# Gate stage: h added to e*gate by accumulating transfers, upper frames turned by VectorE, tiles finished one pair later

## The chip, the cores and the metric

The kernel runs on one core of a Trainium2 chip. The metric is device time in microseconds (us) of one execution. A core has five engines with an instruction queue each: TensorE (PE, with its weight loads shown as PEld), VectorE (DVE), ScalarE (ACT), GpSimd (POOL) and SyncE (SP). SP only issues transfers (DMAs); POOL issues transfers and computes as well. An engine works through its queue in order, so an instruction that waits also holds whatever stands behind it.

## The reference

One layer of a streaming encoder step over 2048 prompt frames and 32 sample frames of 1024 channels. The stage that is changed here is the last one, the gated embedding and the final norm:

```python
h = h + jnp.concatenate([yA, yB], axis=-1) @ w_out
gate = jax.nn.sigmoid(rmsnorm(h, g_ple) @ w_ple_gate)
h = h + (p @ w_ple) * gate
...
return rmsnorm(h, g_final), ...
```

All arithmetic is fp32.

## The kernel before

**Stages.** The input projection comes first, then the mixers and the output projection, then what is left of the embedding e = p·W_ple, and last the gate stage. The rows of h and of e go to device memory (`h_d`, `e_d`) and are read back by the gate stage.

**Products.** An fp32 product is done as three products in the format fp32r. `split` makes two parts of an operand: ACT copies it to fp32r (L81), and DVE subtracts that copy from the operand (L84). Two tiles of 128 frames form a pair, and a pair's [256 x 1024] times the weights' [1024 x 1024] is done as a 2x2 block matrix in seven block products (`seven`), each of 12 matmuls with a 512-wide result. Their operands are the blocks 11, 12 and 22 and the sums S1 to S4 on the side of the frames. PE does them in this order: 11, 12, S2, S1, S3, S4, 22. S1 adds the two blocks of the lower frames, S2 subtracts block 11 from S1, S3 is 11 minus 21, and S4 is 12 minus S2.

**The gate stage.** There are 16 tiles of prompt frames in eight pairs, i = 0, 2, ... 14, and tile 16 with the 32 sample frames, which runs after pair 4 ("short gate"). Pair 14 has a loop body of its own, `last_pair`. For each pair the stage needs:

- the frames turned, channels onto partitions (`prep_g`). The lower tile i+1 is loaded by quarters (four DMAs, L1512), so that a 32x32 block transposition of DVE (L1560) is all that is left to do. The upper tile i is loaded whole; ACT copies it into `ho` (L1552) and PE transposes it in eight matmuls into the PSUM tile `pth` (L1554). The sums and the splits follow (L1743, L84, L81).
- the results (`gate_ops`): ACT copies a result out of PSUM (L1573), DVE adds the second product to it (L1581), ACT takes the sigmoid (L1582, or L1579 straight from PSUM). Then DVE multiplies half a row block of e by the gate (L1584) and adds it to h (L1585).
- the finish (`done_g`): ACT squares h and sums it (L94), POOL makes the reciprocal root out of that (L73, L77), DVE scales h by it and by the final weights (L1592), and the tile is stored (L1593) by POOL for the tiles up to 5 and tile 16, else by SP.

**Buffers.** Two rings of four [128 x 1024] buffers serve the stage. `ya` holds e's rows and the frames that are to be turned (`hn`); `xh` holds h's rows. `ring4` takes the next buffer of a ring; a load into it waits until the buffer's last user is done, a store included.

**Order.** Between the seven products of pair i lie steps 1 to 6. Pair i+2 is prepared in them: at step 2 the lower frames are turned, at step 3 (step 4 for two of the pairs) the rest is made. Within what the buffers and the data allow, a scheduler places the instructions of each engine by its own estimate of the times; what is marked `keep_in_program_order` stays where the program has it. So the real order on an engine isn't that of the text, and it is shown below where it matters.

## Time and profile before

| | us |
|---|---|
| median of three runs | 911.79 (911.69 to 913.55) |
| profiled execution, its own time | 909.97 |
| its span | 908.2 |
| input projection, mixers | 0 to about 535 |
| output projection | about 535 to 705 |
| rest of the embedding | 705 to 729.5 |
| gate stage on PE | 729.5 to 900.5 |
| work after PE's last matmul | 900.5 to 908.2 |

The clock granted to PE is 0.998 of full speed in the mean. "T6" below stands for the time at which PE starts pair 6, and so on for the other pairs; in the execution before, T6 is 797.90. "T6+16.3" is 16.3 us after it.

In a row of a timeline the columns are the start, the length, the engine, the line of the kernel, the operation, result and operands, shapes and the number of instructions in the row; brackets at its end show the idle time before it and what ended that. The lengths of neighbouring instructions overlap a little, since an engine starts one while the last is draining; what one costs the engine is the distance from start to start. In a row of a group, the number of instructions stands behind the x, then the busy time and the mean in ns.

### The profile page before, as it was taken

What the parts mean: (1) busy time and instruction counts of PE and PEld (TensorE: products, weight loads), DVE (VectorE), ACT (ScalarE), POOL (GpSimd) and SP (SyncE); (2) the same over time, 40 slices, a digit from 0 to 9 for tenths busy, and PEclk for the clock granted to TensorE, in tenths of its full rate; (3) what the DMA queues carried; (4) which work ended last, traced back from release to release, by engine and by line L of the source; (5) the groups of instructions that cost most, each with busy time, mean ns of one, the idle gap of its engine ahead of it and who ended that gap; (6) DMA issues with size and microseconds to landing.
All of it is one profiled execution on the core that took longest, in us unless ns stands there. A gap on an engine that the chain in (4) does not pass through costs nothing.

```text
span 908.2 us, 12176 instructions
## 1 busy us (share of the span) xinstructions
PE 893.2 (98%) x4174; PEld 722.8 (80%) x4174; DVE 702.4 (77%) x1158; ACT 460.1 (51%) x834; POOL 152.0 (17%) x290
## 2 busy tenths in 40 slices
PE   8999999999999999999999999999999999999996
PEld 6788888888888887877778886888887888778885
DVE  6899799897993688846667579965565988897885
ACT  7744554554453345533444376544434865565554
POOL 2210122222121123100000020221111211120012
PEclk9999999999999999999999999999999999999999
DMA  8255286857699666667745496787677965565554
GB/s 268 63 188 172 84 262 204 246 157 226 179 340 424 176 222 200 215 222 225 264 136 175 163 331 198 255 259 250 199 274 254 342 244 176 184 228 196 185 193 168
DMA packets 113387, 198.52 MB, mean 219 GB/s; under 512 B 13174, under 2 KB 70062, under 8 KB 112429
## 3 DMA queue, kind: packets, MB, share of 16 engines
q1 hardware_dynamic: 91309, 124.72, 42.5%
q0 software_dynamic: 19568, 68.62, 22.2%
q10 hardware_dynamic: 2448, 4.39, 1.3%
q8 instruction: 33, 0.54, 0.3%
q14 instruction: 29, 0.24, 0.1%
HBM read 132.53 MB, written 65.15 MB: 218 GB/s over the span
## 4 chain that ended last, share of the span: by engine, by line
PE 73%; issue 11%; DMA 8%; DVE 3%; ACT 2%; POOL 2%; POOLq 0%; DVEq 0%; ACTq 0%
PE x_g L185 9%; PE x_o L185 8%; PE x_zab L646 6%; PE x_zbv L646 6%; PE x_ch L646 6%; PE z_g L185 5%; PE z_o L185 4%; DMA raw_zab_0b<-in_w_in_dram 4%; PE z_zab L646 3%; PE z_ch L646 3%; PE z_zbv L646 3%; PE e L109 2%; PE y_g L185 2%; PE y_o L185 2%; DMA B<-p_d 2%
## 5 line engine op out<-in xcount | busy, mean ns | idle before, releaser
L185 PE MATMUL z_o<-wo,y_S 128*128 128x512 f32 x192 | 47.4, 389 | 0.0
L185 PE MATMUL x_o<-wo_T,y_S 128*128 128x512 f32 x192 | 46.4, 391 | 0.6 <-DVE c_o L1319 0.6
L646 PE MATMUL x_zab<-B,w_zab_S 128*128 128x512 f32 x192 | 46.8, 392 | 0.2 <-DVE w_zab_S L84 0.2
L185 PE MATMUL z_g<-wg,g_S 128*128 128x512 f32 x192 | 46.8, 391 | 0.0
L646 PE MATMUL z_zab<-B,w_zab_S 128*128 128x512 f32 x192 | 46.8, 391 | 0.0
L185 PE MATMUL x_o<-wo,y 128*128 128x512 f32 x192 | 45.2, 390 | 0.0
L646 PEld LDWEIGHTS x_zab<-B,w_zab_S 128*128 128x128 f32 x192 | 35.8, 188 | 8.8 <-DVE w_zab_S L84 0.6
L185 PEld LDWEIGHTS x_o<-wo_T,y_S 128*128 128x128 f32 x192 | 35.9, 188 | 8.7 <-DVE c_o L1319 1.3
L185 PEld LDWEIGHTS x_o<-wo,y 128*128 128x128 f32 x192 | 36.1, 188 | 7.7
L646 PEld LDWEIGHTS z_zab<-B,w_zab_S 128*128 128x128 f32 x192 | 35.8, 188 | 7.8 <-DVE w_zab_S L84 0.3
L185 PEld LDWEIGHTS z_o<-wo,y_S 128*128 128x128 f32 x192 | 36.0, 188 | 7.5
L646 PE MATMUL x_ch<-B,w_ch_S 128*128 128x512 f32 x168 | 41.9, 393 | 0.0
L185 PEld LDWEIGHTS z_g<-wg,g_S 128*128 128x128 f32 x192 | 35.8, 188 | 7.5 <-ACT c_g L1573 0.2
L646 PE MATMUL x_zbv<-B,w_zbv_S 128*128 128x512 f32 x168 | 40.9, 393 | 0.3 <-ACT zs L986 0.3
L646 PE MATMUL z_zbv<-B,w_zbv_S 128*128 128x512 f32 x168 | 40.5, 390 | 0.0
L646 PE MATMUL z_ch<-B,w_ch_S 128*128 128x512 f32 x168 | 40.4, 390 | 0.0
L646 PEld LDWEIGHTS x_zbv<-B,w_zbv_S 128*128 128x128 f32 x168 | 31.3, 188 | 8.0 <-ACT zs L986 0.7
L646 PEld LDWEIGHTS x_ch<-B,w_ch_S 128*128 128x128 f32 x168 | 31.3, 188 | 7.3 <-ACT U L986 0.4
L646 PEld LDWEIGHTS z_ch<-B,w_ch_S 128*128 128x128 f32 x168 | 31.6, 188 | 6.6
L646 PEld LDWEIGHTS z_zbv<-B,w_zbv_S 128*128 128x128 f32 x168 | 31.5, 188 | 6.5
L81 ACT CAST y_S<-y_fS 128x512 fp32r<-128x512 f32 x28 | 17.0, 620 | 28.1 <-PE x_o L185 12.2
L1319 DVE TENSOR_TENSOR c_o<-x_o,x 128x512 f32<-128x512 f32 x14 | 9.6, 689 | 21.8 <-PE x_o L185 21.8
(552 smaller groups left out, 2288.9 us busy)
## 6 DMA issues: line engine op xcount, KB each, us to landing
wn<-in_w_in_dram SPq DMA_DIRECT2D x24, 512.0 KB, 4.8
y<-y_d SPq DMA_DIRECT2D x16, 512.0 KB, 6.8
p_dT<-T POOLq DMA_DIRECT2D x15, 512.0 KB, 5.1
e<-e_d SPq DMA_DIRECT2D x15, 512.0 KB, 4.1
x<-in_x_prompt_dram SPq DMA_DIRECT2D x14, 512.0 KB, 5.6
B<-p_d POOLq DMA_DIRECT2D x3, 2048.0 KB, 15.6
B<-p_dT POOLq DMA_DIRECT2D x3, 2048.0 KB, 21.5
h_d<-x SPq DMA_DIRECT2D x12, 512.0 KB, 7.1
```

Of the source, the lines that this page charges most:

```text
L81: ins = nc.scalar.copy(hi, src)
L109: nc.tensor.matmul(ps, pps[:, a, k], wp[k][b][:, cs], start=k + q == 0, stop=k == 1 and q == 2)
L185: nc.tensor.matmul(ps[:n], lhs[:, k, a, :n], w[b][:, k], start=start and k + q == 0, stop=k == KH - 1 and q == 2, skip_group_check=True)
L646: nc.tensor.matmul(ps, lhs[:, k, x], b[:, k, y], start=start and k + q == 0, stop=stop and k == KH - 1 and q == 2, skip_group_check=True)
L1319: add = lambda o, a, b: nc.vector.tensor_tensor(o, a, b, op=ALU.add)
```

## The change

- h's rows are not loaded any more for the pairs 0 to 12, and DVE's 28 adds (L1585 before) are gone. When both halves of a tile of e have been multiplied by the gate, POOL issues a transfer that reads the tile's 512 KB of h from `h_d` and adds them to e in place (L1590 after, `accum_op`).
- A tile is finished on e's buffer, and a pair's two tiles are finished during the next pair, at its steps 3 and 5 (in the last pair at the steps 2 and 3). `done_g`'s square and scaling are now held in program order.
- Tiles 0 to 11 and 16 are stored by POOL, tiles 12 to 15 by SP; before, SP stored the tiles from 6 on.
- e's rows of the pairs 0 to 12 move to the ring `xh`. That ring now holds a tile from the load of e to the store of the finished rows one pair later.
- The upper frames are loaded by quarters and turned by DVE as the lower ones are. ACT's copies `ho` and PE's transposes of the prompt tiles are gone. The first pair is included.
- The loads of the next pair's frames move to step 1.

```diff
-        def by_quarters(i):
+        def by_quarters(i, pool=ya):
...
-            first_h = load_rows(xh, "hn", 0, h_d)
+            first_h = by_quarters(0, xh)
...
-                ee, hh = half_of(e, at, n), half_of(h, at, n)
+                ee = half_of(e, at, n)
                 nc.vector.tensor_tensor(ee, ee, c[:n], op=ALU.mult)
-                nc.vector.tensor_tensor(hh, hh, ee, op=ALU.add)
+                if h is not None:
+                    hh = half_of(h, at, n)
+                    nc.vector.tensor_tensor(hh, hh, ee, op=ALU.add)
+                elif at[0] + at[1] == 1:
+                    r = tiles[i + at[0]][0]
+                    nc.gpsimd.dma_start(e[at[0]], h_d[r:r + P], accum_op=ALU.add)
...
-            nc.vector.scalar_tensor_tensor(h[:n], h[:n], rf[:n], g_bc[:n], op0=ALU.mult, op1=ALU.mult)
-            (nc.sync if 6 <= i < NT - 1 else nc.gpsimd).dma_start(rows_of(y_p, y_s, r, n), h[:n])
+            ins = nc.vector.scalar_tensor_tensor(h[:n], h[:n], rf[:n], g_bc[:n], op0=ALU.mult, op1=ALU.mult)
+            if later:
+                tc.keep_in_program_order(ins)
+            (nc.sync if NT - 5 <= i < NT - 1 else nc.gpsimd).dma_start(rows_of(y_p, y_s, r, n), h[:n])
...
-                got["upper"] = load_rows(ya, "hn", i, h_d) if i else first_h
+                got["upper"] = by_quarters(i) if i else first_h
...
+            def sooner():
                 if not ahead:
                     load()
-                lower.extend(turned_here(got["lower"], not i))
+
+            def first():
+                if not got:
+                    load()
+                lower.extend(turned_here(got["lower"], True))
...
-                a11, a12 = turned(i, got["upper"])
-                put("11", a11)
+                a11, a12 = turned_here(got["upper"], True)
+                put("11", a11, whole)
...
-            return {2: first, 4 if i in (2, 8) else 3: second}
+            return {1: sooner, 2: first, 4 if i in (2, 8) else 3: second}
...
-            h = [load_rows(xh, "h", i + b, h_d, queue=nc.gpsimd if i < 6 else nc.sync) for b in range(2)]
-            e = [load_rows(ya, "e", i + b, e_d) for b in range(2)]
-            seven(f"g{i}", A, W, *gate_ops(h, e, P, f"g{i}", i), following)
-            done_g(i, h[0])
+            e = [load_rows(xh, "e", i + b, e_d) for b in range(2)]
+            if i:
+                following = joined(following, finish)
+            seven(f"g{i}", A, W, *gate_ops(None, e, P, f"g{i}", i), following)
+            finish = {st: lambda b=b, i=i, e=e: done_g(i + b, e[b], True) for b, st in enumerate((3, 5))}
             if i in (0, 2, 4):
                 next(short_steps)
-            if i + 2 < NT - 3:
-                done_g(i + 1, h[1])
-        last_pair(NT - 3, S[NT - 3], lambda: done_g(NT - 4, h[1], True))
+        last_pair(NT - 3, S[NT - 3], finish[3], finish[5])
```

Three places show how the order moves. The first is DVE in pair 6, from the end of the short gate to the first split of pair 8. The names: `c_g6_11` is the gate of pair 6's block (1,1), `hn_9` and `hn_8` are the lower and the upper frames of pair 8, `g8_11` is its operand 11 (low part), `g8_fS1` the sum S1. A row "TENSOR_SCALAR e_3" is the finish of tile 3, and "TENSOR_TENSOR e_5<-e_5,c_g4_11" a multiplication of tile 5 by the gate. Before:

```order
L1581 TENSOR_TENSOR c_g6_00_7193<-y_g6_7179,c_g6_00_7193 128x512
L1560 STREAM_TRANSPOSE hn_9_7211<-hn_9_7211 128x1024
L1592 TENSOR_SCALAR h_16_6917<-h_16_6917,rstd_f16_7158,g_bc_89 32x1024
L1592 TENSOR_SCALAR h_5_6931<-h_5_6931,rstd_f5_7166,g_bc_89 128x1024
L1584 TENSOR_TENSOR e_6_7174<-e_6_7174,c_g6_00_7193 128x512
L1743 TENSOR_TENSOR g8_fS1_7247<-hn_9_7211 128x512
L1585 TENSOR_TENSOR h_6_7170<-h_6_7170,e_6_7174 128x512
L84 TENSOR_TENSOR g8_11_7263<-pth_8_0_7249,g8_11_7263 128x4x128
```

After, in the same stretch of DVE:

```order
L1584 TENSOR_TENSOR e_5_6873<-e_5_6873,c_g4_11_6982 128x512
L1597 TENSOR_SCALAR e_3_6682<-e_3_6682,rstd_f3_7003,g_bc_89 128x1024
L1584 TENSOR_TENSOR e_5_6873<-e_5_6873,g_g4_10_7035 128x512
L1581 TENSOR_TENSOR c_g6_11_7177<-x_g6_7100,c_g6_11_7177 128x512
L1581 TENSOR_TENSOR c_g6_01_7155<-z_g6_7102,c_g6_01_7155 128x512
L1584 TENSOR_TENSOR e_6_7096<-e_6_7096,c_g6_00_7115 128x512
L1560 STREAM_TRANSPOSE hn_9_7117<-hn_9_7117 128x1024
L1597 TENSOR_SCALAR e_4_6871<-e_4_6871,rstd_f4_7161,g_bc_89 128x1024
L1750 TENSOR_TENSOR g8_fS1_7179<-hn_9_7117 128x512
L1560 STREAM_TRANSPOSE hn_8_7122<-hn_8_7122 128x1024
L1584 TENSOR_TENSOR e_7_7098<-e_7_7098,c_g6_11_7177 128x512
L1750 TENSOR_TENSOR g8_fS2_7185<-g8_fS1_7179,hn_8_7122 128x512
```

The split of `g8_11` comes next. What was eight rows behind the first result of pair 6 now stands behind the results (1,1) and (0,1), behind the multiplications of the tiles 5, 6 and 7 and behind the finishes of the tiles 3 and 4.

The second place is POOL in the same pair. Its rows are the stores (L1600), the accumulating transfers (L1590) and the small steps of the roots (L73, L77). After:

```order
L1600 DMA out_0_dram<-e_2_6680 128x1024
L73 TENSOR_SCALAR ms_f16_7090<-ssq_f16_7088 32x1
L77 TENSOR_TENSOR rstd_f16_7092<-ms_f16_7090,nhalf_83 32x1
L1600 DMA out_1_dram<-h_16_6867 32x1024
L73 TENSOR_SCALAR ms_f4_7159<-ssq_f4_7157 128x1
L77 TENSOR_TENSOR rstd_f4_7161<-ms_f4_7159,nhalf_83 128x1
L1600 DMA out_0_dram<-e_3_6682 128x1024
L1590 DMA e_5_6873<-h_d_58 128x1024
L1600 DMA out_0_dram<-e_4_6871 128x1024
L73 TENSOR_SCALAR ms_f5_7226<-ssq_f5_7224 128x1
```

The sample rows take one place in the ring `xh`, which shifts it by one: the load of e's tile 5 follows the store of tile 2, that of tile 6 the store of tile 16, that of tile 7 the store of tile 3, and from there on the load of tile k+4 the store of tile k. All these stores are rows of POOL, and an accumulating transfer stands in one queue with them.

The third place is SP from the last preparation on. Before:

```order
L396 DMA e_14_7900<-e_d_59 128x1024
L396 DMA h_14_7902<-h_d_58 128x1024
L396 DMA h_15_7904<-h_d_58 128x1024
L129 DMA pps_l_7898<-pp_d_65 128x512
L123 DMA wl_0_0_7925<-wl_d00_61 128x1024
```

After:

```order
L396 DMA e_14_7770<-e_d_59 128x1024
L396 DMA e_10_7432<-e_d_59 128x1024
L396 DMA e_11_7434<-e_d_59 128x1024
L396 DMA e_12_7600<-e_d_59 128x1024
L396 DMA e_13_7602<-e_d_59 128x1024
L129 DMA pps_l_7768<-pp_d_65 128x512
L123 DMA wl_0_0_7795<-wl_d00_61 128x1024
L123 DMA wl_0_1_7796<-wl_d01_62 128x1024
L123 DMA wl_1_0_7799<-wl_d10_63 128x1024
L123 DMA wl_1_1_7800<-wl_d11_64 128x1024
L396 DMA h_14_7772<-h_d_58 128x1024
L396 DMA h_15_7774<-h_d_58 128x1024
```

The loads of h for the last pair move behind the loads of its other operands (`pps_l`, `wl`); their buffers are those of the tiles 10 and 11, which are stored in the last pair itself.

More of the change, by code (lines that the diff above doesn't have):

```diff
@@ L1611, in short_ops, with last_pair @@
             return carry, out
-        def last_pair(i, A, before):
+        def last_pair(i, A, sooner, before):
             pps = load_pps(ss.tile([P, 2, 2, P], F32R, tag="s", name="pps_l"), i + 1, nc.sync)
@@ L1728, in end @@
                 normed(1, root(1))
-            seven(f"g{i}", A, W, held, out, {1: chunk, 3: before, 4: rest, 5: upper_half}, first_tile=True, end=end)
+            seven(f"g{i}", A, W, held, out, {1: chunk, 2: sooner, 3: before, 4: rest, 5: upper_half}, first_tile=True, end=end)
         def prep_g(i, ahead=False):
@@ L1739, in put, with comb @@
                 split(view(A[q][:, :, 0]), view(A[q][:, :, 1]), src)
-            def comb(q, x, y, op, view=lambda t: t):
-                t = ss.tile([P, KH, P], F32, tag="s", name=f"g{i}_f{q}")
-                nc.vector.tensor_tensor(view(t), x, y, op=op)
+            def comb(q, x, y, op):
+                t = whole(ss.tile([P, KH, P], F32, tag="s", name=f"g{i}_f{q}"))
+                nc.vector.tensor_tensor(t, x, y, op=op)
                 return t
@@ L1749, in load @@
                 got["lower"] = by_quarters(i + 1) if i else first_lower
[L1750 removed]
+                got["upper"] = by_quarters(i) if i else first_h
             if ahead:
                 load()
[L1755 removed]
+            def sooner():
                 if not ahead:
                     load()
[L1758 removed]
+            def first():
+                if not got:
+                    load()
+                lower.extend(turned_here(got["lower"], True))
             def second():
                 a21, a22 = lower
[L1762 to L1764 removed]
+                s1 = comb("S1", a21, a22, ALU.add)
+                a11, a12 = turned_here(got["upper"], True)
+                put("11", a11, whole)
                 s2 = comb("S2", s1, a11, ALU.subtract)
[L1766 to L1768 removed]
+                s3 = comb("S3", a11, a21, ALU.subtract)
+                put("12", a12, whole)
+                put("S2", s2, whole)
                 s4 = comb("S4", a12, s2, ALU.subtract)
[L1770 to L1772 removed]
+                put("S1", s1, whole)
+                put("S3", s3, whole)
+                put("S4", s4, whole)
                 put("22", a22, whole)
             S[i] = A
[L1776 removed]
+            return {1: sooner, 2: first, 4 if i in (2, 8) else 3: second}
         S = {}
@@ L1806, in short_gate, with joined, both, run @@
             yield
+        def joined(a, b):
+            def both(p, q):
+                def run():
+                    p()
+                    q()
+                return run
+            return {**a, **{st: both(a[st], f) if st in a else f for st, f in b.items()}}
         short_steps = short_gate()
```

10 lines of the change are left out of this document (1 added, 9 removed).

## The prediction

> **What bounds the kernel now.** I read the page's busy shares first, then the stage's windows, PE's timeline in a pair, the groups of the gate stage, and the transfers.
>
> ```profile
> PE 893.2 (98%) x4174; PEld 722.8 (80%) x4174; DVE 702.4 (77%) x1158; ACT 460.1 (51%) x834; POOL 152.0 (17%) x290
> ```
>
> PE bounds the whole span. One row per pair of the gate stage gives length, then busy time of PE, PEld, DVE, ACT and POOL, the granted clock, the share of the DMA engines and GB/s:
>
> ```profile
> 797.90:817.80 19.90, 19.90 (x92) 16.32 (x91) 18.19 (x28) 12.66 (x22) 4.23 (x7) 1.00 0.69 231
> 817.80:837.90 20.10, 20.10 (x94) 16.71 (x94) 14.89 (x22) 9.22 (x17) 1.98 (x4) 1.00 0.59 212
> 837.90:858.00 20.10, 20.10 (x94) 16.53 (x93) 17.05 (x25) 11.70 (x21) 2.07 (x4) 1.00 0.58 210
> 858.00:878.30 20.30, 20.30 (x96) 16.78 (x94) 15.94 (x24) 10.36 (x20) 2.15 (x4) 1.00 0.50 173
> ```
>
> PE is busy through every pair at full clock, DVE for 15 to 18 of 20 us. So in this stage the time is what PE executes, plus whatever PE comes to wait for. Between pairs lies one piece of other work, the short gate:
>
> ```profile
> 790.53 1.08 PE L337 MATMUL x_gl<-wg,gl_a 128*64 128x512 f32 x4
> 797.90 2.90 PE L185 MATMUL x_g<-wg,g 128*128 128x512 f32 x12
> ...
> 803.36 2.88 PE L185 MATMUL x_g<-wq,g_S 128*128 128x512 f32 x12
> 806.08 2.88 PE L185 MATMUL z_g<-wg,g_S 128*128 128x512 f32 x12
> 808.81 1.03 PE L1554 MATMUL pth<-ident,ho 128*128 128x128 f32 x8
> 809.60 3.02 PE L185 MATMUL x_g<-wg_T,g_S 128*128 128x512 f32 x12
> ...
> 878.06 0.63 PE L185 MATMUL x_g<-wg,g 128*128 128x512 f32 x2
> ```
>
> A block product takes 2.72 us from start to start (803.36 to 806.08), seven take 19.04. From T6 = 797.90 to T14 = 878.06, four pairs take 20.04 each. The short gate covers 7.4 us ahead of T6.
>
> **The gain.** The difference, 1.00 us a pair, is PE's transposition of the upper frames (0.79 from start to start in the rows above, the rest in the products around it). The groups of the stage:
>
> ```profile
> L1554 PE MATMUL pth<-ident,ho 128*128 128x128 f32 x56 | 7.4, 274 | 0.0
> L1585 DVE TENSOR_TENSOR h<-h,e 128x512 f32<-128x512 f32 x28 | 18.8, 685 | 0.8 <-DMA h<-h_d 0.6
> L1592 DVE SCALAR_TENSOR_TENSOR h<-h,rstd_f,g_bc 128x1024 f32<-128x1024 f32 x14 | 18.0, 1283 | 9.2 <-POOL rstd_f L77 9.2
> L94 ACT ACTIVATE junk<-h 128x1024 bf16<-128x1024 f32 x14 | 14.8, 1057 | 4.3 <-DVE h L1585 2.2 <-issue 2.0
> L1560 DVE STREAM_TRANSPOSE hn<-hn 128x1024 f32<-128x1024 f32 x7 | 8.7, 1238 | 0.0
> L1552 ACT COPY ho<-hn 128x512 f32<-128x512 f32 x14 | 8.1, 619 | 3.1 <-DMA hn<-h_d 3.1
> L1573 ACT COPY c_g<-x_g 128x512 f32<-128x512 f32 x16 | 9.2, 577 | 4.7 <-PE x_g L185 4.7
> L1582 ACT ACTIVATE c_g<-c_g,rs_h 128x512 f32<-128x512 f32 x21 | 14.7, 718 | 15.2 <-DVE c_g L1581 15.2
> L81 ACT CAST g_S<-g_fS 128x512 fp32r<-128x512 f32 x30 | 17.3, 617 | 13.4 <-DVE g_fS L1743 13.4
> L77 POOL TENSOR_TENSOR rstd_f<-ms_f,nhalf 128x1 f32<-128x1 f32 x14 | 8.1, 576 | 1.1
> L73 POOL TENSOR_SCALAR ms_f<-ssq_f 128x1 f32<-128x1 f32 x14 | 6.4, 455 | 110.1 <-ACT junk L94 110.0
> ```
>
> Seven groups of eight matmuls lie in these 56, an eighth at the start of the stage; all go, so −8.0 us on PE (0.79 each would be −6.3, the lower end). On DVE a pair loses four additions and gains one transposition, on ACT it loses two copies; neither engine bounds the stage, so this brings nothing by itself. Both frames come by quarters now, so SP issues three more transfers a pair (24 with the first), and drops eight of its ten loads of h and six of its eight stores. POOL drops 6 loads of h, gains 14 accumulating transfers, and stores 13 tiles instead of 7. SP's and POOL's issuing is a cost only through what waits behind it.
>
> **The new waits.** Steps on DVE cost this from start to start:
>
> ```profile
> 824.33 1.28 DVE L1592 SCALAR_TENSOR_TENSOR h<-h,rstd_f,g_bc 128x1024 f32<-128x1024 f32 x1 [0.72 <-POOL rstd_f L77]
> 825.53 0.68 DVE L1581 TENSOR_TENSOR c_g<-y_g,c_g 128x512 f32<-128x512 f32 x1
> ...
> 827.61 1.24 DVE L1560 STREAM_TRANSPOSE hn<-hn 128x1024 f32<-128x1024 f32 x1
> 828.77 0.65 DVE L1585 TENSOR_TENSOR h<-h,e 128x512 f32<-128x512 f32 x1
> ...
> 833.34 0.68 DVE L1743 TENSOR_TENSOR g_fS<-g_fS,pth 128x512 f32<-128x512 f32 x1
> 833.94 0.68 DVE L1743 TENSOR_TENSOR g_fS<-pth,hn 128x512 f32<-128x512 f32 x1
> ```
>
> A finish costs 1.2, a transposition 1.16, any operation on half a tile 0.6. The transfers, with the KB of one and the median us from issue to landing:
>
> ```profile
> e<-e_d SPq DMA_DIRECT2D x15, 512.0 KB, 4.1
> ...
> h<-h_d POOLq DMA_DIRECT2D x6, 512.0 KB, 5.2
> out_dram<-h POOLq DMA_DIRECT2D x6, 512.0 KB, 3.6
> e_d<-eout POOLq DMA_DIRECT2D x2, 512.0 KB, 5.8
> ```
>
> A buffer of `xh` becomes free when its tile is stored, and only then is the next e loaded. One round trip r is a store of POOL, 3.6, a load, 4.1, and 0.2 of handing over: 7.9. Before, the loads ran a pair ahead; now the trip lies behind a finish that is itself made a pair later. The accumulating transfer (L) isn't in the trace. Its nearest row is POOL's plain load of the same 512 KB of h, 5.2, which I take; POOL's store, 3.6, is the low end, twice the load, 10.4, the high one, since it has to read the tile it adds to.
>
> *Pair 6 to 8.* PE ends the short gate at T6. Behind its last product ACT has a copy, a sigmoid and two casts (0.6 to 0.7 each) and the square of tile 2 (1.06). Then come POOL's root (0.46 + 0.58) and DVE's finish (1.2): T6+6. Ahead of the store POOL's queue also holds the root of tile 3. I put the store at T6+7.0. Tile 5 of e is there at 7.0+r. In the order after, DVE then has: multiply tile 5 (0.6), finish tile 3 (1.2), whose store goes out at T6+8.9+r and whose buffer tile 7 of e needs. Tile 7 lands at 8.9+2r; multiplication, S2 and the split of `g8_11` (0.6 each) make it 10.8+2r with the handover to PE. Pair 8 should start at 19.04, so PE waits 2r−8.2. There is a second path, over the multiplication of tile 5: ACT's copy of the next result uses the gate's buffer that it frees, PE's S4 product waits for that copy (8.3+r), ends 2.72 later, and 7.1 us of DVE rows follow up to the split: 18.2+r, a wait of r−0.8. At r = 7.9 the first decides: **+7.6**. Even with no transfer late, S4 ends at T6+16.3 and the same 7.1 us follow (three results and products 1.8, two transpositions 2.3, one finish 1.2, three more 1.8): a floor of +4.6. Before, `g8_11` stood ahead of these results.
>
> The pairs 0 to 4 have no predecessor in the ring or only an early one. At T4 the preparation of pair 6 ends about T4+21.2 by the same rows, and the short gate keeps PE until T4+26.4: nothing. In the pairs 8 and 10 the preparation stands ahead of the late rows: nothing.
>
> *Pair 12 to 14.* Tile 8 is finished at about T12+6.3: sigmoid, two casts with their splits, square, root, finish, 5.4 by the rows, and some handovers. Its store goes out at 6.4, tile 12 of e lands at 6.4+r; DVE then has five operations of 0.6 (three of them the last sums and the split), two transpositions and another result, 6.0 in all: 12.4+r against 19.04, so r−6.6, **+1.3**.
>
> *The last pair.* Before, its own h was loaded long ahead:
>
> ```profile
> 891.02 0.69 DVE L1634 TENSOR_TENSOR h<-h,c_g 128x512 f32<-128x512 f32 x1
> ...
> 894.99 0.69 DVE L1670 TENSOR_TENSOR c_g<-x_g,c_g 128x512 f32<-128x512 f32 x1
> ...
> 900.58 0.42 DVE L1633 TENSOR_TENSOR g_l<-e_l,g_l 128x256 f32<-128x256 f32 x1 [0.39 <-PE e_l L109]
> ```
>
> The first addition came at T14+13.0, the last result was added up by T14+17.5 (895.60), and PE's last four short products follow that. Now the rows of h wait for the store of tile 10, which is finished at about T14+8.5, so they land at 8.6+r = 16.5. There is also the square of tile 13, on ACT ahead of the copy that PE's S4 product needs. The accumulating transfer of tile 13 goes out at T14+7.1, square and copy follow it, so S4 starts at 8.9+L and its result is added at 12.3+L = 17.5. The later of the two counts. Behind it DVE has that addition, two finishes and two more operations: 4.2 to 17.5+4.2 = 21.7 instead of 17.5, **+4.2**. In general the term is max(8.6+r, 12.3+L)−13.3; that is 3.2 with r alone.
>
> **The sum:** −8.0 + 7.6 + 1.3 + 4.2 = +5.1. On the profiled execution, 909.97, that is 915.1. The median of the runs stands 1.8 above that execution, so for it I forecast 911.79 + 5.1 = **916.9**.
>
> **Rivals.** *Light transfers, no change.* The single landings in this stage spread widely:
>
> ```profile
> DMA to landing us min/median/max: 2.3/3.9/6.9
> ```
>
> If stores and accumulating transfers came near the light end, some 3.3 us each, with r = 6.7, pair 8 would wait 5.9 (second path), pair 14 0.1, the end 8.6+6.7−13.3 = 2.0 or, by L, 12.3+3.3−13.3 = 2.3: −8.0+5.9+0.1+2.3 = +0.3, or 912.1. For it: the DMA engines are busy for 0.50 to 0.69 of these pairs, and most loads of h leave SP. Against: the medians above come from the same stage at the same traffic. The Trainium skill, DMA: Bandwidth & Descriptors, section "Anatomy of one DMA — SWDGE (gpsimd) path", gives 2.0 us plus bytes over 436e3 per us for a transfer issued by GpSimd, which for 512 KB would be an estimated 3.2 us and bring the sum to about zero; the trace's medians of 3.6 to 5.8 on POOL's queue lie above it, so I keep the trace's.
>
> *Faster.* The place is POOL's stores of the tiles 2, 8 and 10. If they went out 3 us earlier than I count (the handovers and the root ahead of them are my weakest numbers), pair 8 would wait the floor, 4.6, pair 14 nothing, the end max(13.5, 14.5)−13.3 = 1.2: −8.0+4.6+1.2 = −2.2, or 909.6. From there on it is faster by more than 0.2%, which is 1.8 us and about what a measurement of this kernel can tell from no change. Against: the floor rests on the order and on PE's own times.
>
> *The accumulating transfer is slow.* At L = 10.4, the square of tile 5 on ACT, which stands ahead of the cast of `g8_11`, decides: its multiplications end at T6+9.5+r, and L, the square, cast and split (2.3) follow, so pair 8 waits r+L−7.3 = 11.0, and the end waits 9.4: −8.0+11.0+1.3+9.4 = +13.7, or 925.5. For it: it reads and writes the tile. Against: POOL's other transfers of this size land in 3.6 to 5.8. The Trainium skill, SBUF — State Buffer, section "SBUF: two separate sides", says that a VectorE operation in a two-port mode keeps GpSimd from writing the descriptors of its transfers; POOL's stores land sooner here (3.6) than the loads of SP (4.1) with DVE busy for 17 of 20 us, so the trace shows none of it.
>
> **How the numbers follow.** The forecast's own case (two to three waits of this size, 914 to 922) 0.56; light transfers 0.15; faster 0.11; slow accumulating transfer 0.12; another wait that I don't see, slower, 0.06. Faster by over 0.2%: 0.11, within 0.2% 0.15, slower 0.74. The range 910.5 to 927 leaves out most of the faster case and what lies above the slow transfer.
>
> **What would show it.** No `pth` of 128x128 in the gate stage, and pairs of 19.04 us on PE wherever nothing waits. An idle PE of 7 to 8 us ahead of pair 8, with DVE waiting for transfers of e's tiles 5 and 7; about 1 ahead of pair 14; an end of the last pair that is some 4 us longer. L is read as the time from issue to landing of the accumulating transfer. I am wrong if PE goes from pair 6 to 8 without a gap, if L is near 10 or more, or if a wait opens in the pairs 0 to 4.

## The result and the profile after

The changed kernel takes 943.53 us in the median (940.25 to 946.42), the kernel before 912.08 beside it: 1.034 times as long, 95% interval 1.0314 to 1.0366. The forecast, 916.9 with a range to 927.0, had the direction, but a sixth of the size: +5.1 us where +31 were measured. The profiled execution after is the longest of the six, 946.42 with a span of 944.6, 36.4 us above the span before.

The page's busy shares and the transfers of the gate stage, as they stand now:

```profile
PE 900.6 (95%) x4110; PEld 723.0 (77%) x4110; DVE 695.2 (74%) x1138; ACT 453.0 (48%) x818; POOL 165.3 (17%) x304
```

```profile
e<-e_d SPq DMA_DIRECT2D x15, 512.0 KB, 4.4
hn<-h_d SPq DMA_DIRECT2D x57, 128.0 KB, 5.8
e<-h_d POOLq DMA_DIRECT2D x14, 512.0 KB, 6.9
out_dram<-e POOLq DMA_DIRECT2D x12, 512.0 KB, 5.1
```

Two things are to be seen. PE has 64 matmuls fewer, 8.0 us by the prediction's count, and is busy 7.4 us longer: its other matmuls took some 15 us more in all. And it stands idle for 944.6−900.6 = 44.0 us where it was 15.0, 29 more. So 29 us of waits and 15 us of slow matmuls, less 8, make up the 36. In the median the accumulating transfers land after 6.9 us, POOL's stores after 5.1 instead of 3.6, the quarters of the frames after 5.8 instead of 2.9.

Where the time went, pair by pair. T is the start of a pair as PE would have it without waits inside its first two products (the start of its third product less 5.44 us); pair 4 includes the short gate:

| stretch | before | after | more | the prediction had |
|---|---|---|---|---|
| start to T0 | 729.5 | 736.7 | +7.2 | −1 |
| T0 to T2 | 20.0 | 19.0 | −1.0 | −1.0 |
| T2 to T4 | 21.1 | 19.9 | −1.2 | −1.0 |
| T4 to T6 | 27.4 | 32.0 | +4.6 | −1.0 |
| T6 to T8 | 20.2 | 31.1 | +10.9 | +6.6 |
| T8 to T10 | 19.9 | 19.4 | −0.5 | −1.0 |
| T10 to T12 | 20.1 | 21.1 | +1.0 | −1.0 |
| T12 to T14 | 20.0 | 24.6 | +4.6 | +0.3 |
| T14 to the end | 30.1 | 40.7 | +10.6 | +4.2 |

**Pair 6 to 8** is the place that the prediction worked out in most detail. The rows of the timeline after, of POOL, SP, DVE, ACT and PE (start, length, engine):

```profile
813.69 0.62 POOL L1600 DMA_DIRECT2D out_dram<-e  x1
816.82 0.34 SPq L396 DMA_DIRECT2D e<-e_d  x1
821.49 0.69 DVE L1584 TENSOR_TENSOR e<-e,c_g 128x512 f32<-128x512 f32 x1 [3.42 <-DMA e<-e_d]
822.27 0.59 ACT L1573 COPY c_g<-z_g 128x512 f32<-128x512 f32 x1 [4.63 <-DVE e L1584]
822.91 3.01 PE L185 MATMUL z_g<-wg,g_S 128*128 128x512 f32 x12 [1.73 <-ACT c_g L1573]
823.68 0.63 POOL L1600 DMA_DIRECT2D out_dram<-e  x1 [3.82 <-DVE e L1597]
824.31 0.91 POOL L1590 DMA_DIRECT2D e<-h_d  x1
828.82 0.34 SPq L396 DMA_DIRECT2D e<-e_d  x1
832.93 1.22 PE L185 MATMUL x_g<-wg,g 128*128 128x512 f32 x2 [4.29 <-ACT g L81]
835.13 0.69 DVE L1584 TENSOR_TENSOR e<-e,c_g 128x512 f32<-128x512 f32 x1 [3.40 <-DMA e<-e_d]
837.08 4.63 PE L185 MATMUL x_g<-wg,g 128*128 128x512 f32 x10 [2.07 <-DVE g L84]
```

The chain is the one foretold. The store of tile 2 (813.69) lets the load of e's tile 5 go (816.82), its multiplication follows at 821.49: the first round trip took 7.8 us. The store of tile 3 (823.68) lets tile 7 go at 828.82, and it is multiplied at 835.13: the second took 11.4, with an accumulating transfer issued right behind the store. Its store took 5.1 us (to 828.82) and what follows 6.3, where 3.6 and 4.1 had been taken. The two paths over S4 and over `g8_11` are both there as waits of PE: 1.73 at 822.91, and 4.29 and 2.07 for the two parts of `g8_11` at 832.93 and 837.08. The 4.29 ends with ACT's cast, which stands behind the square of tile 5, and that square waited for its accumulating transfer: the path of the rival with the slow transfer. DVE had turned the upper frames only 0.5 us before that cast, so this path added no more than that.

**Pair 4 to 6** was put down as free of waits:

```profile
780.12 1.77 POOL L1590 DMA_DIRECT2D e<-h_d  x2
781.78 0.67 POOL L1600 DMA_DIRECT2D out_dram<-e  x1
791.30 0.34 SPq L396 DMA_DIRECT2D e<-e_d  x1
795.38 0.69 DVE L1584 TENSOR_TENSOR e<-e,c_g 128x512 f32<-128x512 f32 x1 [5.21 <-DMA e<-e_d]
803.90 1.29 PE L337 MATMUL x_gl<-wg,gl_a 128*64 128x512 f32 x4 [3.56 <-DVE c_gl L1608]
```

The load of e's tile 4 needs the buffer of tile 1. That tile's store stands behind two accumulating transfers in POOL's queue and is done 9.5 us after its issue (781.78 to 791.30). The trip is 13.6 us, DVE waits for it, and the short gate, which was to cover the preparation, itself waits for a row of DVE behind it.

**Pair 12 to 14** lost 4.6 us by a trip of the same kind. POOL stores tile 8 at 885.64; tile 12, which takes its buffer, is multiplied 11.3 us later:

```profile
896.92 0.69 DVE L1584 TENSOR_TENSOR e<-e,c_g 128x512 f32<-128x512 f32 x1 [7.60 <-DMA e<-e_d]
899.40 4.62 PE L185 MATMUL x_g<-wq,g 128*128 128x512 f32 x12 [3.74 <-DVE c_g L1581]
```

PE's wait stands ahead of the last product of pair 12, which waits for a result that DVE adds behind that multiplication; the prediction had it ahead of pair 14. Pair 10, put down as free, has two smaller waits of PE around its end, 0.94 and 0.45.

**Slow matmuls.** The columns of the windows are length, busy time of PE, PEld, DVE, ACT, POOL, granted clock, DMA share, GB/s:

```profile
832.90:837.00 4.10, 2.08 (x4) 1.16 (x4) 1.87 (x4) 1.04 (x3) 0.40 (x1) 0.50 0.57 201
837.00:842.00 5.00, 4.92 (x12) 3.85 (x13) 4.84 (x8) 1.47 (x4) 0.00 (x0) 0.50 0.35 109
842.00:855.00 13.00, 13.00 (x58) 10.75 (x57) 9.63 (x14) 5.88 (x11) 2.40 (x3) 0.99 0.86 211
...
899.40:904.00 4.60, 4.60 (x13) 3.64 (x14) 4.60 (x8) 3.58 (x7) 0.00 (x0) 0.63 0.02 9
904.00:917.80 13.80, 10.90 (x49) 8.68 (x47) 9.35 (x14) 7.07 (x13) 4.77 (x9) 0.98 0.80 216
917.80:921.70 3.90, 2.08 (x4) 1.16 (x4) 0.00 (x0) 1.65 (x4) 1.35 (x4) 0.50 0.98 362
921.70:927.10 5.40, 5.35 (x13) 4.25 (x14) 0.00 (x0) 0.00 (x0) 0.45 (x1) 0.50 0.58 209
```

After such a gap PE doesn't start again at full clock: it is granted about half for some 3 to 4 us, and for 5 behind the second of two gaps (the windows from 837.0 and 921.7). The ten matmuls at 837.08 take 4.4 us from start to start; at full clock, with 2.72 for twelve, ten take 2.3. The prediction had no such term.

**The last pair.** SP, ACT and PE, in order of time:

```profile
906.35 6.18 SPq L123 DMA_DIRECT2D wl<-wl_d  x4
916.21 1.06 ACT L94 ACTIVATE junk<-e 128x1024 bf16<-128x1024 f32 x1 [4.84 <-DMA e<-h_d]
917.26 0.57 ACT L1573 COPY c_g<-x_g 128x512 f32<-128x512 f32 x1
917.88 2.08 PE L185 MATMUL x_g<-wg_T,g_S 128*128 128x512 f32 x4 [2.98 <-ACT c_g L1573]
920.07 1.06 ACT L94 ACTIVATE junk<-e 128x1024 bf16<-128x1024 f32 x1 [2.24 <-DMA e<-h_d]
921.13 0.57 ACT L1573 COPY c_g<-z_g 128x512 f32<-128x512 f32 x1
```

Both squares wait for their accumulating transfers, and the two copies behind them are those that PE's products S3 (917.88, a gap of 2.98) and S4 (921.75, 1.79) wait for. POOL issued the transfers at 907.98 and 910.54, 8.2 and 9.5 us before the squares began. They ran beside the four loads of `wl`, 512 KB each, which SP issues from 906.35 on; in the window from 917.8 the DMA engines are busy for 0.98.

### The profile page after: what moved, and what is told of

Its sections match the earlier page's. It is cut to its first block, busy times and chain, and to the rows that moved or that the text cites. A ratio compares the mean times of both kernels' runs of the same rounds, so it can differ in the third digit from the quotient of the medians.

```text
span 944.6 us, 12042 instructions
## 1 busy us (share of the span) xinstructions
PE 900.6 (95%) x4110; PEld 723.0 (77%) x4110; DVE 695.2 (74%) x1138; ACT 453.0 (48%) x818; POOL 165.3 (17%) x304
## 5 line engine op out<-in xcount | busy, mean ns | idle before, releaser
L185 PE MATMUL z_g<-wg,g_S 128*128 128x512 f32 x192 | 49.2, 406 | 3.5 <-ACT c_g L1573 3.5
L1584 DVE TENSOR_TENSOR e<-e,c_g 128x512 f32<-128x512 f32 x21 | 14.2, 685 | 31.9 <-DMA e<-e_d 28.7
L185 PE MATMUL x_g<-wg,g 128*128 128x512 f32 x96 | 27.3, 433 | 6.4 <-ACT g L81 4.3
```

Source lines behind the costliest of these rows:

```text
L185: nc.tensor.matmul(ps[:n], lhs[:, k, a, :n], w[b][:, k], start=start and k + q == 0, stop=k == KH - 1 and q == 2, skip_group_check=True)
L1584: nc.vector.tensor_tensor(ee, ee, c[:n], op=ALU.mult)
```

## The experiments

Each verdict is against the kernel before, timed on the same chip in the same stretch; its median lay between 910.6 and 912.2 us. Where no other figure is given, the number in brackets is the 95% interval of the ratio.

### Which part carries the loss

**The upper frames alone (e1).** The change's part on the upper frames is put into the kernel before:

```diff
-                got["upper"] = load_rows(ya, "hn", i, h_d) if i else first_h
+                got["upper"] = by_quarters(i) if i else first_h
...
-                a11, a12 = turned(i, got["upper"])
+                a11, a12 = turned_here(got["upper"], True)
```

> The kernel before with one part of the change alone: the upper frames are loaded by quarters and turned by VectorE, pair 0 included; h is loaded and added, and tiles are finished, as before. Theory A (the loss comes from e's buffers, which wait for stores of the next pair): the gate stage gains 1.0 us a pair, 8.0 in all, and loses about 4 ahead of pair 0, where PE waits for transfers that stand behind the quarters of the first upper tile in SP's queue: about 908. Theory B (the quarter loads crowd SP's queue and hold the stage): slower than before, 918 or more, with PE waiting in the pairs.

Measured: 937.51 us against 911.21, a ratio of 1.029 (1.0261 to 1.0313). This part, which I had booked as pure gain, loses 26 us by itself, as theory B has it. It isn't quite the part as the change has it: here the frames are loaded at step 2 as before, there at step 1.

**The same but for pair 0 (e2).**

> As the one with the upper frames alone, but pair 0's upper tile is loaded whole and turned by PE as before. If the wait ahead of pair 0 comes from the three more transfers at that place, it goes: about 905, some 3 us below the other, and PE starts pair 0 at 729.5 again. If it comes from elsewhere, the two are equal but for the 0.8 us of PE's transposition.

Measured: 931.27, 1.022 (1.0198 to 1.0234), 6 us less than e1. PE's part of the embedding, from its first product to T0, takes 23.8 us in e1 and 24.9 in e2, so the three transfers of the first tile are not where the 6 us lie: T0 differs by 1.5, and most of the rest falls on pair 2 (25.3 to 19.9 us), whose order of DVE changed too. That expectation failed.

The cause shows in e1 itself, between the pairs 8 and 10:

```profile
840.32 3.18 SPq L1512 DMA_DIRECT2D hn<-h_d  x6
854.05 1.28 DVE L1592 SCALAR_TENSOR_TENSOR h<-h,rstd_f,g_bc 128x1024 f32<-128x1024 f32 x1 [0.72 <-POOL rstd_f L77]
855.25 1.24 DVE L1560 STREAM_TRANSPOSE hn<-hn 128x1024 f32<-128x1024 f32 x1
857.19 1.22 PE L185 MATMUL x_g<-wg,g 128*128 128x512 f32 x2 [8.50 <-ACT g L81]
```

The quarters are issued by 843.5, but the planner has put the turning of the upper frames behind both finishes of pair 8. In DVE's order the split of `g10_11` stands 15 and 12 rows behind the results (1,1) and (0,1); before, it stands 8 and 9 rows ahead of them. PE waits 8.5 us for the operand.

**The quarters in ACT's queue (e5).** Against e2:

```diff
-                got["upper"] = by_quarters(i) if i else first_h
+                got["upper"] = by_quarters(i, queue=nc.scalar) if i else first_h
```

> As the kernel with the upper frames turned by VectorE but for pair 0, and the quarters of the upper tile are issued by ACT instead of SP. The arithmetic and the buffers are the same. Theory D (the transposition by VectorE cost so much because its loads stood in SP's queue, and the planner put the turning behind the pair's results): the preparation of each pair stands ahead of the result (1,1) again, PE goes from pair to pair without a gap, seven pairs gain 1.0 each: 903 to 907. Theory E (VectorE's own extra time, or the 128 KB transfers themselves, cost it): no better than before, 911 or more.

Measured: 924.61 against 912.24, 1.015 (1.0128 to 1.0168). E2's loss falls from 20 to 12 us with one word, and the order comes back: the split of `g10_11` stands ahead of both results again. So the queue was a cause, as theory D has it, but not the only one; the time lies in theory E's range. What is left are waits like this, in e5's timeline:

```profile
774.05 4.62 PE L185 MATMUL x_g<-wq,g 128*128 128x512 f32 x12 [3.11 <-DVE c_g L1581]
845.13 4.56 PE L185 MATMUL x_g<-wq,g 128*128 128x512 f32 x12 [3.12 <-DVE c_g L1581]
```

PE's product 22 waits for a result that DVE adds only behind the preparation, which is now longer (theory E's part; that this is why the result is late is argued from the order, and no run isolates it), and both times the product then runs at reduced clock.

**The rest of the change without the upper frames (e3).** The upper frames are loaded whole and turned by PE as before; the diff is that of e1 the other way round.

> The changed kernel with the upper frames loaded whole and turned by PE as before; accumulating transfers, finish in the next pair and buffers as in the change. Theory A: nearly all of the loss stays, 940 to 948, with PE's gaps around pairs 6, 8 and 14. Theory B: 915 or less.

Measured: 934.16, 1.026 (1.0236 to 1.0277), between the two theories. Each of the two halves of the change alone costs 23 to 26 us, both together 31, but not in the same pairs. T4 to T6 is 33.6 us here, T6 to T8 25.1, the end 35.5. e1 loses its time mostly in the pairs 2, 8 and 12 (25.3, 30.7 and 27.4 us) and none at the end; the changed kernel, which loads the frames a step earlier, has 19.9 and 19.4 in the pairs 2 and 8. So e1's 26 us are not what the upper frames cost in the changed kernel. That is the distance from e3 to it, 9 us instead of a gain of 8: in the profiled executions T6 to T8 is 6.0 us longer than in e3, T12 to T14 3.9, the end 5.3, while every other pair is 0.5 to 1.7 shorter.

### The accumulating transfers

**Finished in the same pair (e4).**

```diff
-            finish = {st: lambda b=b, i=i, e=e: done_g(i + b, e[b], True) for b, st in enumerate((3, 5))}
+            done_g(i, e[0])
+            if i + 2 < NT - 3:
+                done_g(i + 1, e[1])
+            finish = {3: lambda: None, 5: lambda e=e: done_g(NT - 4, e[1], True)}
```

(and `finish` is not joined to the steps of the next pair any more.)

> The changed kernel with one thing undone: a pair's tiles are finished directly behind their pair, not at the next pair's steps. The accumulating transfers and e's buffers stay as they are. Theory A (buffers held too long): the stores come some 8 us earlier, the loads of e with them, and most gaps close: 915 to 925. Theory C (the accumulating transfers and POOL's queue make the round trip long, wherever the finish stands): 935 or more.

Measured: 938.71, 1.029 (1.0261 to 1.0316). The gain against the changed kernel is 5 us, in theory C's range; theory A asked for some 20. That the finish comes a pair later is not the main cause. PE's waits are spread over all pairs but the first now, for results on DVE or ACT's copies of them.

**The transfer without the addition (e6).** It writes h over e, so the sum is left out; every engine's order is that of the changed kernel.

```diff
-                    nc.gpsimd.dma_start(e[at[0]], h_d[r:r + P], accum_op=ALU.add)
+                    nc.gpsimd.dma_start(e[at[0]], h_d[r:r + P])
```

> The changed kernel with the addition left out of the accumulating transfers: the same 14 transfers write h's rows over e, in the same queue and order, so that the output is h and not h + e*gate. Every instruction order is that of the changed kernel. Theory F (the addition makes the transfer long, 6.9 us instead of about 5, and the waits with it): 6 to 12 us less than the changed kernel, 931 to 937. Theory G (the place and the queue cost it, whatever the transfer does): within 3 of it, 941 to 946.

Measured: 934.83, 1.026 (1.0229 to 1.0296), 9 us less than the changed kernel, as theory F has it.

**Eight rows instead of 128 (e10).** Again every order is the same:

```diff
-                    nc.gpsimd.dma_start(e[at[0]], h_d[r:r + P], accum_op=ALU.add)
+                    nc.gpsimd.dma_start(e[at[0]][:8], h_d[r:r + 8], accum_op=ALU.add)
```

> The changed kernel, but each accumulating transfer moves 8 rows instead of 128 (32 KB instead of 512): the same instructions in the same order with the same waits; h is left out of the sum for all other rows. Theory J (the bytes of the transfer cost it, its length and what it takes from the stores and loads beside it): 915 to 922, near the kernel without transfers. Theory K (the dependence and the place in POOL's queue cost it): 930 or more, near the kernel with the plain transfers.

Measured: 921.58 against 911.01, 1.012 (1.0090 to 1.0140), at the upper end of theory J's range.

**No transfer (e7).** The `elif` with the transfer is taken out; the order changes a little.

> The changed kernel without its 14 accumulating transfers: h is left out of the sum for the tiles 0 to 13. What is left of the loss are the buffers held until the next pair's stores, the quarters in SP's queue and the order. Theory A (held buffers): 925 to 935, still with gaps ahead of the pairs 6 and 8. Theory F or G (the transfers carry the loss): 905 to 915.

Measured: 917.12, 1.007 (1.0043 to 1.0090), between the two ranges and nearer to that of F and G.

The transfers in the three of them, with KB and us to landing, e6 first, then e10 (e7 has none), and below it the stores of e7:

```profile
e<-h_d POOLq DMA_DIRECT2D x14, 512.0 KB, 5.3
```

```profile
e<-h_d POOLq DMA_DIRECT2D x14, 32.0 KB, 3.3
```

```profile
out_dram<-e POOLq DMA_DIRECT2D x12, 512.0 KB, 3.4
```

The steps from the changed kernel down are the clearest thing in this study, since every engine's order is the same in the first three: 943.5 with the addition (6.9 us a transfer), 934.8 without it (5.3), 921.6 with a sixteenth of the bytes (3.3), 917.1 with none. So the bytes of the transfer and its addition carry 22 of the 31 us, and the dependence and the place in the queue 4 to 5. About 5 us of the loss remain without any transfer. The profiled executions say the same of the gate stage alone: from T0 to the end of PE's last matmul they take 200.6 us in the changed kernel, 190.0 in e6, 179.9 in e10, 175.0 in e7 and 171.0 before. Pair 4 to 6 shows it best, with 32.0, 28.7, 26.8 and 26.4. Theory J holds against K for the sum, and F against G. The price that the prediction took for the transfer, POOL's plain load with 5.2 us, was right for the plain transfer (5.3) and too low for the accumulating one. The Trainium skill, DMA: Bandwidth & Descriptors, section "Anatomy of one DMA — SWDGE (gpsimd) path", would give an estimated 3.2 us for each 512 KB; the trace has 6.9, 5.3 without the addition, and 3.4 for stores where no such transfer is about.

The last pair is the exception. From T14 to the end of PE's last matmul it takes 33.5 us in the changed kernel, 31.1 in e6, 29.0 in e10, 24.4 in e7 and 22.4 before. Its two transfers land after 8.1 and 9.4 us, without the addition after 7.2 and 7.5, and with 32 KB still after 6.4 and 5.2, each time beside the loads of `wl`. So there the wait for a transfer at that place (theory K) carries more than its addition or its bytes. That the loads of `wl` make the transfers long is the likely reason, and no run has moved them.

**All stores by SP (e8).**

```diff
-            (nc.sync if NT - 5 <= i < NT - 1 else nc.gpsimd).dma_start(rows_of(y_p, y_s, r, n), h[:n])
+            (nc.sync if i < NT - 1 else nc.gpsimd).dma_start(rows_of(y_p, y_s, r, n), h[:n])
```

> The changed kernel with all stores of the prompt tiles issued by SP, so that a store doesn't stand behind an accumulating transfer in POOL's queue. Theory H (the round trip is long because stores queue behind accumulating transfers): the store's time falls from 5.1 to about 3.5 and the kernel gains 4 us or more, 940 or less. Rival: in SP's queue the stores hold the loads that stand behind them: 945 or more.

Measured: 943.40, 1.035 (1.0323 to 1.0380), no different from the changed kernel and between the two ranges. The stores did become fast (3.0 us in the median), so half of theory H is right, but the time came back at other places: T12 to T14 is 25.1 us and the end 43.4, with a single wait of 7.2 us for ACT's copy behind the squares, and the accumulating transfers took 7.9.

### What a gap costs

**Waits put in by hand (e9).** Into the kernel before:

```diff
                 s1 = comb("S1", a21, a22, ALU.add, whole)
+                for _ in range({4: 3, 8: 5, 10: 7, 12: 9}.get(i, 0)):
+                    nc.vector.tensor_tensor(s1, s1, s1, op=ALU.max)
```

> The kernel before with waits put in by hand: ahead of the sums of pairs 4, 8, 10 and 12 VectorE has 3, 5, 7 and 9 more operations of 0.6 us (each takes the maximum of S1 with itself, so that nothing is changed). Theory I (a gap of PE costs more than its length, since the granted clock falls to half after one of some 2.5 us): the products behind a short gap take 2.72 us as ever, those behind a longer gap 4.2 or more, and the kernel loses 1.5 us or more beyond its gaps. Rival: 12 matmuls take 2.72 us behind every gap, and the loss is the sum of the gaps.

Measured: 924.53 (two runs), 1.014 (1.0117 to 1.0170). PE's rows behind the largest gap, and the windows around it and around the last one:

```profile
850.96 1.22 PE L185 MATMUL x_g<-wq,g_S 128*128 128x512 f32 x2 [4.07 <-ACT g_S L81]
851.98 1.05 PE L185 MATMUL z_g<-wg,g_S 128*128 128x512 f32 x2
852.83 3.13 PE L185 MATMUL x_g<-wq,g_S 128*128 128x512 f32 x10
855.80 2.43 PE L185 MATMUL z_g<-wg,g_S 128*128 128x512 f32 x10
```

```profile
850.90:855.00 4.10, 4.04 (x11) 3.04 (x12) 4.10 (x7) 1.56 (x4) 0.00 (x0) 0.59 0.81 268
855.00:860.00 5.00, 5.00 (x28) 4.24 (x27) 4.96 (x9) 3.75 (x8) 0.00 (x0) 1.00 0.98 347
...
892.30:897.00 4.70, 4.67 (x15) 3.74 (x16) 4.17 (x7) 2.36 (x5) 0.00 (x0) 0.69 0.30 118
```

Behind the gap of 4.07 us the clock is 0.59 over the next 4.1 us, a loss of 1.7; behind three gaps of 1.28, 0.87 and 1.43 in a row it is 0.69 over 4.7 us, another 1.5. Of the 12.2 us by which the gate stage and its end grew (190.9 to 178.7), 8.3 are gaps and 3.9 aren't. Theory I holds in kind. Across all profiles of this study, 12 matmuls behind a single gap of up to 1.78 us took 3.0 to 3.3 us, but once 4.5 (behind 1.64, in e1); behind gaps of 1.81 to 3.12 mostly 4.2 to 4.6, but three times 3.0 (behind 2.61, 2.89 and 3.11); behind 3.7 and more always 4.4 or more. So the length of a gap alone doesn't decide it. Two gaps of 1.57 and 0.55 us in a row brought the clock to 0.65 over 4.5 us in e15, and 1.49 and 0.55 in e14 left it at 1.00; what else counts stays open. The Trainium skill, TensorE: Matmul & The Clock Gate, section "Part 1: The HAM clock gate (the "warmup" mystery)", has this rule: after an idle window of some 3.4 us the clock falls to half, and it takes about as long to be released. The length of the slow stretch agrees; the gaps that set it off begin lower here, at 1.6 to 1.8 us.

### Is the gain real

**Two additions by GpSimd (e11) and one (e12).** In the kernel with ACT's queue, to take off DVE what it had gained; e11 loads the frames one step earlier too:

```diff
-                nc.vector.tensor_tensor(hh, hh, ee, op=ALU.add)
+                (nc.gpsimd if n == P and at[0] == at[1] else nc.vector).tensor_tensor(hh, hh, ee, op=ALU.add)
```

> The kernel before with the upper frames of pairs 2 to 14 turned by VectorE, their quarters issued by ACT, the loads one step earlier, and two of the four additions of h a pair (blocks (0,0) and (1,1)) made by GpSimd. Theory L (what was left of the loss in the ACT-queue kernel is VectorE's time between the results and the next preparation, 1.2 us more a pair): the gaps ahead of the product 22 close, 903 to 908. Rival: GpSimd's additions, 1.3 us each, are late or slow VectorE, and it stays at 915 or more.

> As the kernel with the upper frames turned by VectorE and their quarters issued by ACT, and one addition of h a pair, that of block (0,0), made by GpSimd. Theory L: half of the gaps ahead of the product 22 go, 908 to 918. Rival: no change against that kernel, 922 or more.

Measured: e11 917.20, 1.006 (1.0046 to 1.0082); e12 927.29, 1.017 (1.0150 to 1.0192), no better than e5. Both lie in their rival's range. In e11 the pairs 8 and 10 take 19.0 and 19.1 us, the gain whole; the loss sits in the pairs 0, 4 and 6. In pair 0, ACT stands for 6.0 us behind the copy of the sample frames, whose load is late in SP's queue.

**Only some pairs on VectorE (e13, e14, e15).** Upper frames of the pairs 10 and 12, then 4 as well, then 14 as well, the additions of the pair ahead on GpSimd:

```diff
-                got["upper"] = load_rows(ya, "hn", i, h_d) if i else first_h
+                got["upper"] = (by_quarters(i, queue=nc.scalar) if i in DV else load_rows(ya, "hn", i, h_d)) if i else first_h
```

> The kernel before with the upper frames of the pairs 10 and 12 alone turned by VectorE (quarters issued by ACT), and the additions of the blocks (0,0) and (1,1) of the pairs 8 and 10 made by GpSimd. If the gain of 1.0 us a pair is real: 909 to 910, the pairs 8 and 10 take 19.04 us on PE. If VectorE's longer preparation gives it back: equal to the kernel before or slower, 911 to 914.

> The same with pair 4 as well (and GpSimd's additions in pair 2). Gain real: 908 to 909, three pairs of 19.04. Given back: 911 to 915.

> The same with the pairs 4, 10, 12 and 14. Gain real and no wait ahead of pair 14: 907 to 908. A wait ahead of pair 14 as in the kernel with all pairs on VectorE (20.9 us there): 909 to 911.

Measured: 917.06 (1.0054, 1.0036 to 1.0071), 913.89 (1.0026, 1.0013 to 1.0039), 915.65 (1.0043, 1.0027 to 1.0058). All slower, e13 and e15 by more than either of their two cases, e14 within "given back". Pair 2 gains 1.2 us in e14 (21.1 to 19.9), but pair 8 takes 23.0 instead of 19.9, with three waits:

```profile
834.66 0.73 PE L185 MATMUL x_g<-wg,g 128*128 128x512 f32 x2 [1.49 <-ACT g L81]
835.94 2.56 PE L185 MATMUL x_g<-wg,g 128*128 128x512 f32 x10 [0.55 <-DVE g L84]
839.56 3.02 PE L185 MATMUL x_g<-wq,g 128*128 128x512 f32 x12 [1.05 <-DVE c_g L1583]
```

**The same with the loads one step earlier (e16, e17).**

```diff
-            return {2: first, 4 if i in (2, 8) else 3: second}
+            return {**({1: sooner} if i in DV else {}), 2: first, 4 if i in (2, 8) else 3: second}
```

> The kernel of e14 (the upper frames of the pairs 4, 10 and 12 turned by VectorE, two additions a pair of the pairs 2, 8 and 10 on GpSimd) with the loads of these pairs' frames one step earlier. Gain real, lateness was the cause: the pairs 2, 8 and 10 take 19.0 to 19.9 us, 908 to 909, faster than the kernel before by 0.3%. If VectorE's time gives it back wherever the loads stand: 911 or more.

> The same with pair 14 as well: 907 to 909 if the wait ahead of pair 14 goes too, 909 to 911 if it stays (20.9 us in e11).

Measured: e16 910.87, a ratio of 1.0003 (0.9983 to 1.0022), no change; e17 909.03 against 910.55, 0.9976 (0.9962 to 0.9989). Pair 8 takes 19.0 us in both, so the lateness was the cause there. e17 is faster than the kernel before, by 0.24%: of four pairs at 1.0 us, 1.5 us are left. Its time lies where its two ranges meet, and the wait ahead of pair 14 stayed. PE's waits in its gate stage:

```profile
814.97 3.06 PE L185 MATMUL x_g<-wq,g 128*128 128x512 f32 x12 [0.27 <-DVE c_g L1583]
852.75 3.01 PE L185 MATMUL x_g<-wq,g 128*128 128x512 f32 x12 [0.27 <-DVE c_g L1583]
873.67 3.04 PE L185 MATMUL x_g<-wq,g 128*128 128x512 f32 x12 [1.56 <-DVE c_g L1583]
```

The last, ahead of pair 14, is the only one over 0.3 us.

## Why the prediction was wrong

The sum came out 31 us too low in the profile (36.4 measured, 5.1 forecast). By place that is 8.2 us ahead of T0, 5.6 in pair 4, 4.3 in pair 6, 2.5 in the pairs 8 and 10, 4.3 in pair 12 and 6.4 in the last pair; the pairs 0 and 2 came as foretold. The steps that failed are the prices of the transfers: r = 7.9 and L = 5.2 were taken from a trace without accumulating transfers, and with them the trips that held PE up took 11.3 to 13.6 us (one stayed at 7.8) and the transfers 5.2 to 9.4. Pair 4 and the clock behind a gap were put at nothing. One by one:

- **The gain of 8.0 us**: right in size. Where nothing waits, a pair takes 19.0 us (T0 to T2 after; the pairs 8 and 10 of e11; pair 8 of e17). The step that failed is the sentence behind it, that neither DVE nor ACT bounds the stage, "so this brings nothing by itself", and that SP's and POOL's issuing costs only "through what waits behind it". I counted the transfers and followed what waited in a few places only. Against e3 the upper frames cost the changed kernel 9 us instead of bringing 8; in the kernel before they cost 26 (e1), and 12 with their quarters in ACT's queue and pair 0 left as it was (e5). There, quarters late in the plan put the preparation behind the pair's results (e1), and with the order restored PE still waits for results that DVE adds behind the longer preparation (e5).
- **Pair 6 to 8, +7.6**: the chain held, row for row. The store of tile 2 came at T6+6.05 (7.0 foretold), the first trip took 7.8 us (7.9), the second 11.4. With these the formula gives 6.05+3.8+7.8+11.4 = 29.1 less 19.04, a wait of 10.0; that and about 2 us of reduced clock are the 12.0 us by which T6 to T8 exceeds 19.04. The failing term is r for a store with an accumulating transfer beside it.
- **"The pairs 0 to 4 have no predecessor in the ring or only an early one"**: wrong, and a wait there was one of the prediction's own signs of being wrong. Tile 4's load waited for tile 1's store, 13.6 us in all, since two accumulating transfers stood ahead of it. With 32 KB in each of these (e10) the stretch takes 26.8 us instead of 32.0.
- **Pair 12 to 14, +1.3**: the store of tile 8 came at T12+6.4 as foretold; the trip took 11.3 us instead of 7.9. The formula gives 4.7 with it, 5.6 was measured, and PE's product 22 ahead of pair 14 ran at a clock of 0.63.
- **The last pair, +4.2**: the path over the squares decided, as foretold, with L of 8.2 and 9.5 instead of 5.2. Its formula gives 8.5 with 9.5; the rest to 10.6 is again the clock (0.50 in the windows from 917.8 to 927.1). L was mis-sized, and the missing addition is the smaller part of that: the plain transfers at this place took 7.2 and 7.5 (e6), where the median of all 14 is 5.3. The median of a stage was the wrong price for a place where 2 MB of other loads run.
- **What was missing altogether**: the price of a gap beyond its length. About 15 of the 36 us in the profile are matmuls at reduced clock. The trace before, with 15.0 us of idle time in the whole span, hardly shows one.
- **T0, +7.2 where I had −1**: about half lies in the output projection, where both kernels have the same instructions in the same order; such waits of up to 2.9 us there come and go between the profiles, e1's at 664.09 and e5's without any. The other half lies in the embedding, where PE waited 0.97 us for weights and 2.89 for `pps`, whose loads stand behind the first tile's quarters. e8 shows 2.60 there too; e1 shows none, and e6 and e10, with the changed kernel's order, only 0.2. So it isn't the order alone; what decides it stays open.
- **The rivals**: the slow accumulating transfer, at L = 10.4 with 925.5, came nearest. "Light transfers" and "faster" didn't happen (the floor of 4.6 in "faster" comes out at 4.4 from its own rows). The range ended at 927 because each mechanism was priced alone; several came together, and the clock on top.

## What to carry to other kernels

- A buffer that waits for its own store has a round trip in the path, and its price must be taken for the traffic that the change brings, not for that of the trace before: here 7.9 us became 11 to 14 where accumulating transfers ran beside the store or ahead of it.
- A planner that thinks a load late moves everything that depends on it; before counting a moved load as free, look in the new order at which of PE's operands now stands behind which result. One other queue was worth 7 us here (e2 to e5), one step earlier 2 and 6 us (e14 to e16 and e15 to e17, as ratios to the kernel before).
- Where PE has been busy without a break, a new wait of 2 us or more cost mostly 1.3 to 1.7 us on top here for the clock, with three exceptions; that belongs in the sum.

## What the hardware showed that I hadn't expected

- An accumulating transfer of 512 KB takes 6.9 us in the median, a plain one on the same queue in the same order 5.3, one of 32 KB 3.3, and while accumulating ones of 512 KB are about, other stores on that queue take 5.1 instead of 3.4. Of two accumulating transfers issued within 1.2 us of each other, the first took 5.5 to 6.3 us and the second 9.1 to 9.4 (from 780.1, 845.1 and 863.1 in the profile after); one alone, at 800.4, took 5.2.
- A single gap of 1.8 to 3.1 us mostly, and once three gaps of about 1 us close together, cost the clock: about half is granted for the next 3 to 4 us. Nearly the same gaps passed without it at other times.
- One correction to the text ahead of the prediction: the ring `ya` has five buffers, not four; nothing in the argument hangs on it.
